# Seven block products in place of eight: Strassen's scheme in the second product of a layer's MLP

## The chip, the cores and the metric

The kernel runs on one core of one Trainium2 chip. Five engines work side by side in a core. PE (TensorE) multiplies matrices: an instruction LDWEIGHTS (PEld in the profile) puts a 128x128 block of weights into the array, and a MATMUL streams up to 512 columns past it into PSUM, an accumulation memory of eight banks with 128x512 f32 each. DVE (VectorE), ACT (ScalarE) and POOL (GpSimd) do element by element work, and SP (SyncE) issues most of the transfers from the device's memory into SBUF, the memory that the engines work in. The metric is the device time in microseconds (us), as the median of several runs.

## The reference

Two transformer layers run over 512 latent tokens and 256 context tokens with a width of 1024: layer 0 mixes tokens by differential attention, layer 1 by neighbourhood attention, and each is followed by an MLP. The change is in the MLP of layer 1, which sees the 512 latent tokens only. Cut to what matters:

```python
D_MODEL = 1024
D_FF = 4 * D_MODEL

def squared_relu_mlp(h, w1, w2):
    return jnp.square(jax.nn.relu(h @ w1)) @ w2

x = x + mod_l[5] * squared_relu_mlp(modulate(rms_norm(x, norm2_g[i]), mod_l[3], mod_l[4]),
                                    w_mlp1[i], w_mlp2[i])
```

So the first product is 512x1024 by 1024x4096, the second 512x4096 by 4096x1024, and the gate `mod_l[5]` multiplies the second one's result before it is added to the stream.

## The kernel before

**Arithmetic.** Every f32 operand of a matrix product is split into a high and a low part of type fp32r, and each product is made of three passes (`PASSES`): high by high, high by low, low by high. The split of a weight block is `wsplit` (L140 to L150): ACT copies the raw block `R` into the high half of a tile `W` (L145), and POOL subtracts that from the raw block to get the low half (L146). One block is 128x1024 f32, 512 KB, fetched by SP (`wraw`, L126 to L130) into one of two raw buffers.

**The MLP** (`mlp`, L809 to L892) walks over 16 chunks of 256 hidden features. `up(c)` (L819 to L845) fetches and splits two blocks of w1, and for each of two tiles of 128 features makes 24 matmuls (8 slices of the width by 3 passes) of 512 tokens into a PSUM tile `D0` or `D1`. ACT applies the relu (L838), DVE squares in place (L839), ACT copies the result into the high half of a tile `H` (L841) and DVE forms the low half (L842). `down` (L856 to L878) fetches and splits two blocks of w2, and for each of four tiles of 128 tokens and each of the two halves `n` of the 1024 output columns makes 6 matmuls (2 features tiles by 3 passes) of 512 columns into a PSUM tile `A` or `B`. DVE adds it to a running sum in SBUF (L874 for the first chunk, L876 after it), one of eight pieces 128x512 that lie three to a tile `Q`.

The loop (L880 to L889) makes chunk c+1's `up` and then chunk c's `down`, so that the hidden values of a chunk are ready long before their `down`. The last two chunks go into one `down` with its flag `end` set: before it, `blend` (L847 to L854) multiplies each piece of the running sum by the gate (DVE, L853) and adds it to the stream (L854: POOL for the left half of the columns, DVE for the right one). The last `down` then makes 12 matmuls for each of the eight pieces, DVE multiplies by the gate (L871), adds to the stream (L872), and ACT's queue sends the result out (L1054).

**Buffers** set when work may begin. In this stage there are four `W` buffers (three opened on the left side and one on the right), two raw buffers `R`, four `N` of 128x1024 (one of them holds the gate), four of the eight `H` (the others hold the MLP's input), and in PSUM one `D0`, one `D1`, two `A` and two `B`. A buffer is given out again when the last reader of what was in it is done: the split of the next weight block waits for the matmuls on the one four blocks earlier.

**Order.** In the attention stages the orders on PE, SP and POOL are written out by hand. In the MLP they are not: a planner lays out each engine's instructions ahead of time. It steps through a timeline of its own estimates, and lets an engine take the instruction that stands earliest in the program among those whose inputs and buffers are ready in that timeline. On the chip each engine then runs its list strictly in that order, and an instruction that has to wait holds up all that stand behind it on its engine.

The stage's loop is

```python
        for c in range(nc_ - 2):
            nxt = up(c + 1)
            side()
            down((c,), hid, False)
```

and `side` does nothing in layer 1.

Of the kernel before, what the change touches and what calls it, by code (L numbers as in the profile page):

```python
# [63 lines left out]
class Block:  # L64
    def __init__(self, tc, ctx, a):
        self.tc = tc
        self.nc = tc.nc
        self.a = a
        self.n = 0
        pool = lambda name, bufs, **kw: ctx.enter_context(tc.tile_pool(name=name, bufs=bufs, **kw))  # L70
        self.const = pool("const", 1)
        self.rpool = pool("rpool", 2)
        self.sb = pool("sb", 1)
        self.dram = pool("dram", 1, space=DRAM)
        self.room, self.turns, self.last = {}, {}, {}


    BUFS = {"H": 8, "Q": 8, "E": 2, "X": 2, "Y": 6, "T": 2, "SQ": 12, "SA": 12, "SO": 8, "C4": 1}
# [46 lines left out]

    def wraw(self, src, n):  # L126

        raw = self.rpool.tile([P, 1024], F32, tag="R", name=self._name("R"))[:, :n]
        self.last["SP"] = self.nc.sync.dma_start(raw, src)
        return raw  # L130

# [21 lines left out]
    def mod_load(self, l, n, early=False):  # L153

        src = self.a["wmod"][l, n]
        if early:
            w = self.sbt('M', [P, 2048])
            self.nc.sync.dma_start(w, src)
            ws = [w]
        else:  # L160
            ws = [self.rpool.tile([P, 1024], F32, tag="R", name=self._name("R")) for s in range(2)]
# [647 lines left out]
    def mlp(self, l, t0, xh, hT, tag, mid, done, side):  # L809
        nc = self.nc  # L810
        a = self.a
        ntok = T - P * t0
        c0 = P * t0
        halves = ((0, 384, 0), (384, 768, 512)) if t0 == 0 else ((256, 768, 0),)
        nx = 2 * (NT - t0)
        acc = [self.sbt(tag[0], [P, 3, 512]) for _ in range((nx + 2) // 3)]
        gate = self.load_gates(l, 1, (0, 1) if t0 == 0 else (0,))

        def up(c):  # L819
            w = [self.wload(a["w1"][l, c, s], 1024) for s in range(2)]  # L820
            hid = []
            for f in range(2):
                ps = self.pst(f'D{f}', (P, 1024))

                cuts = [(o, o + 256, o - c0) for o in range(c0, T, 256)] if c == 0 else halves
                for b0, b1, at in cuts:
                    for kt in range(KT):
                        for p, (x, y) in enumerate(PASSES):
                            o = 256 * (kt % 4) + P * f
                            nc.tensor.matmul(ps[:, at:at + b1 - b0], w[kt // 4][:, x, o:o + P],  # L830
                                             hT[kt][:, y, b0:b1],
                                             start=(kt == 0 and p == 0), stop=(kt == KT - 1 and p == 2))
                r = self.sbt('N', [P, ntok])
                if c and t0 == 0:
                    nc.scalar.activation(r.rearrange("p (h n) -> p h n", h=2),  # L835
                                         ps.rearrange("p (h n) -> p h n", h=2)[:, :, :384], AF.Relu)
                else:
                    nc.scalar.activation(r, ps[:, :ntok], AF.Relu)  # L838
                nc.vector.tensor_mul(r, r, r)  # L839
                u = self.sbt(tag[1], [P, 2, ntok], F32R)  # L840
                nc.scalar.activation(u[:, 0, :], r, AF.Copy)  # L841
                nc.vector.scalar_tensor_tensor(u[:, 1, :], r, 1.0, u[:, 0, :].bitcast(F32),  # L842
                                               op0=ALU.mult, op1=ALU.subtract)
                hid.append(u)
            return hid  # L845

        def blend():  # L847

            for i in range(t0, NT):
                for n in range(2):  # L850
                    j = 2 * (i - t0) + n
                    av = acc[j // 3][:, j % 3, :]
                    nc.vector.tensor_mul(av, av, gate[1 if i < 2 else 0][:, 512 * n:512 * n + 512])  # L853
                    (nc.gpsimd, nc.vector)[n].tensor_add(xh[i, n], xh[i, n], av)  # L854

        def down(cs, hid, end):  # L856
            w = [self.wload(a["w2"][l, 2 * c + f], 1024) for c in cs for f in range(2)]
            if end:
                mid()
            for i in range(t0, NT):  # L860
                for n in range(2):
                    ps = self.pst('A' if end else 'AB'[n])
                    for f, hd in enumerate(hid):
                        for p, (x, y) in enumerate(PASSES):
                            nc.tensor.matmul(ps, hd[:, x, P * i - c0:P * i - c0 + P], w[f][:, y, 512 * n:512 * n + 512],  # L865
                                             start=(f == 0 and p == 0), stop=(f == len(hid) - 1 and p == 2))
                    j = 2 * (i - t0) + n
                    av = acc[j // 3][:, j % 3, :]
                    if end:
                        t = self.sbt('T', [P, 512])  # L870
                        nc.vector.tensor_mul(t, ps, gate[1 if i < 2 else 0][:, 512 * n:512 * n + 512])  # L871
                        nc.vector.tensor_add(xh[i, n], xh[i, n], t)  # L872
                    elif cs[0] == 0:
                        nc.vector.tensor_copy(av, ps)  # L874
                    else:
                        nc.vector.tensor_add(av, ps, av)  # L876
                if end:
                    done(i)  # L878

        nc_ = NFF // 2  # L880
        hid = up(0)
        for c in range(nc_ - 2):
            nxt = up(c + 1)
            side()
            down((c,), hid, False)
            side()
            hid = nxt
        hid += up(nc_ - 1)
        blend()  # L889
        down((nc_ - 2, nc_ - 1), hid, True)  # L890


# [40 lines left out]
def hybrid_block(tc, a, out):  # L933
    nc = tc.nc
    with ExitStack() as ctx, ExitStack() as st:
# [19 lines left out]
        with b.psum_phase("psA", **PS_ATTN0):  # L955
# [65 lines left out]
        with b.psum_phase("psC", **PS_ATTN1):  # L1021
# [25 lines left out]
                run(END1, GROUPS1, heads, load, split, **own)  # L1047
            proj["end"]()
            xh1, hT3 = done
        with b.psum_phase("psD", **PS_MLP1):  # L1050

            def done1(i):
                for n in range(2):
                    nc.scalar.dma_start(out[P * (i - 2):P * (i - 1), 512 * n:512 * n + 512], xh1[i, n])  # L1054

            b.mlp(1, 2, xh1, hT3, 'QH', lambda: None, done1, lambda: None)
        b.close("W", "ST", "W", "N", "VM")

# [69 lines left out]
```

## Time and profile before

| | |
|---|---|
| median of 3 runs | 1906.98 us (1906.21 to 1910.55) |
| the profiled execution's own time | 1907.34 us |
| its span, from the first to the last instruction | 1905.4 us |
| PE busy over the span | 94% |
| DVE, ACT, POOL busy over the span | 59%, 44%, 43% |
| mean granted clock of PE | 0.979 |
| layer 1's MLP | from about 1530 us to the end |
| of it the loop, with PE busy without a gap | 1555.5 to 1874.1 us |

The profile gives one execution of the program on the chip. A row of grouped instructions names line, engine, operation and tiles (`W<-R,W` writes a tile W and reads R and W), and then gives the busy time, the mean of one in ns, and the idle time just before them with what ended it. A row of the timeline starts with the time at which the instruction began and its duration, both in us; a bracket gives the idle time before it and what ended that. A busy engine may be one that waits inside an instruction: a duration that is far above others of the same form is such a wait.

### The profile page before, as it was taken

The page shows a single profiled execution, that of the slowest core. Times are in us where ns is not written, and L with a number is a line of the kernel's source. Part 1 is how long each engine was busy: PE and PEld are TensorE (multiplying, and loading weights), DVE is VectorE, ACT ScalarE, POOL GpSimd, SP SyncE. Part 2 cuts the span into 40 slices and gives each one's busy share as a digit, 9 for nine tenths or more (in the row PEclk, how much of TensorE's full clock was granted, in tenths as well). Part 3 has the DMA queues.
Part 4 walks back from the last instruction along what each step waited for, and adds up shares of the span by engine and source line. Part 5 has one row for each costly group of instructions (what it writes and reads, how often), then busy time and mean ns, then how long its engine had stood idle before and what let it go on. Part 6 is the DMA issues. An engine that isn't in the chain of part 4 may idle for free.

```text
span 1905.4 us, 27130 instructions
## 1 busy us (share of the span) xinstructions
PE 1793.9 (94%) x10256; PEld 1570.9 (82%) x10256; DVE 1132.7 (59%) x2158; ACT 829.2 (44%) x1854; POOL 815.6 (43%) x688
## 2 busy tenths in 40 slices
PE   6989999996999999999999998999998989999998
PEld 5878888885789888888888977998898778888886
DVE  4588777785574343343334676778777664444446
ACT  4476767774342212221221245677667342223321
POOL 3655656653224333342442532344335444444443
PEclk9999999997999999999999998999999999999999
DMA  8122222224324343443432132122112323223232
GB/s 327 43 84 78 87 87 87 89 69 159 119 72 140 130 157 111 166 165 112 157 136 73 56 100 64 56 69 84 56 67 89 116 89 99 89 89 107 92 100 77
DMA packets 66499, 197.61 MB, mean 104 GB/s; under 512 B 8192, under 2 KB 23488, under 8 KB 60224
## 3 DMA queue, kind: packets, MB, share of 16 engines
q1 hardware_dynamic: 58608, 186.03, 29.3%
q10 hardware_dynamic: 7760, 9.85, 1.5%
q8 instruction: 80, 1.31, 0.3%
q14 instruction: 51, 0.42, 0.1%
HBM read 180.74 MB, written 15.11 MB: 103 GB/s over the span
## 4 chain that ended last, share of the span: by engine, by line
PE 75%; DVE 11%; ACT 6%; issue 4%; POOL 2%; DMA 2%; ACTq 0%; SPq 0%; POOLq 0%; DVEq 0%
PE PD L830 22%; PE PA L408 14%; PE PA L865 11%; PE PB L865 9%; PE PA L750 4%; PE PA L257 2%; PE PS L517 2%; PE PB L552 2%; PE PB L701 2%; PE PQ L398 1%; PE PS L656 1%; PE PB L686 1%; ACT E L523 1%; PE PB L541 1%; DVE N L311 1%
## 5 line engine op out<-in xcount | busy, mean ns | idle before, releaser
L146 POOL TENSOR_TENSOR W<-R,W 128x1024 fp32r<-128x1024 f32 x142 | 351.3, 2484 | 541.2 <-ACT W L145 541.0
L830 PE MATMUL PD<-Q,W 128*128 128x384 f32 (+2 forms) x1992 | 395.9, 345 | 2.4 <-DVE Q L334 1.1
L830 PEld LDWEIGHTS PD<-Q,W 128*128 128x128 f32 x1992 | 345.7, 188 | 33.7 <-issue 8.6
L145 ACT ACTIVATE W<-R 128x1024 fp32r<-128x1024 f32 (+1 forms) x172 | 172.6, 1021 | 450.5 <-PE PA L865 193.5
L865 PE MATMUL PA<-W,H 128*128 128x512 f32 x1080 | 275.4, 393 | 4.7 <-POOL W L146 3.0
L865 PEld LDWEIGHTS PA<-W,H 128*128 128x128 f32 x1080 | 200.2, 188 | 51.5 <-issue 4.5
L839 DVE TENSOR_TENSOR N<-N 128x768 f32<-128x768 f32 (+1 forms) x64 | 67.0, 1048 | 279.1 <-ACT N L835 170.3
L865 PE MATMUL PB<-W,H 128*128 128x512 f32 x840 | 209.2, 391 | 0.0
L408 PE MATMUL PA<-W,Q 128*128 128x384 f32 (+1 forms) x1008 | 177.4, 331 | 11.2 <-ACT H L446 11.2
L865 PEld LDWEIGHTS PB<-W,H 128*128 128x128 f32 x840 | 157.4, 188 | 33.3
L408 PEld LDWEIGHTS PA<-W,Q 128*128 128x128 f32 x1008 | 163.0, 196 | 12.9 <-ACT H L446 12.9
L296 POOL TENSOR_TENSOR SQ<-SQ,half 128x4 f32<-128x4 f32 (+1 forms) x96 | 99.2, 1034 | 134.0 <-DVE SQ L421 132.9
L842 DVE SCALAR_TENSOR_TENSOR H<-N,H 128x768 fp32r<-128x768 f32 (+1 forms) x64 | 98.1, 1534 | 25.7 <-ACT H L841 25.0
L408 PE MATMUL PA<-WB,H 128*128 128x384 f32 x576 | 108.4, 340 | 0.8 <-DVE Q L469 0.8
L750 PE MATMUL PA<-W,H 128*128 128x512 f32 x384 | 99.1, 409 | 8.0 <-ACT H L743 5.1
L408 PEld LDWEIGHTS PA<-WB,H 128*128 128x128 f32 x576 | 98.6, 188 | 1.8 <-DVE Q L469 1.1
L830 PE MATMUL PD<-H,W 128*128 128x512 f32 (+1 forms) x408 | 94.1, 378 | 2.5 <-DVE SA L290 2.0
L876 DVE TENSOR_TENSOR H<-PA,H 128x512 f32<-128x512 f32 x78 | 53.9, 690 | 69.6 <-PE PA L865 69.6
L750 PEld LDWEIGHTS PA<-W,H 128*128 128x128 f32 x384 | 73.3, 196 | 26.3 <-ACT H L743 5.4
L830 PEld LDWEIGHTS PD<-H,W 128*128 128x128 f32 x408 | 73.8, 188 | 18.0 <-DVE H L334 2.9
L523 ACT ACTIVATE E<-PS,SA 128x768 f32<-128x768 f32 (+1 forms) x96 | 72.8, 759 | 34.6 <-DVE SA L522 31.9
L517 PE MATMUL PS<-Q,Q 128*128 128x256 f32 (+1 forms) x320 | 69.1, 348 | 19.4 <-ACT Q L446 10.3
(210 smaller groups left out, 3056.5 us busy)
## 6 DMA issues: line engine op xcount, KB each, us to landing
R<-in_w_dram SPq DMA_DIRECT2D x128, 512.0 KB
M<-in_wmod_dram SPq DMA_DIRECT2D x48, 1024.0 KB
R<-in_wqa_dram SPq DMA_DIRECT2D x32, 384.0 KB
R<-in_wqb_dram SPq DMA_DIRECT2D x32, 384.0 KB
Y<-in_rpb_dram SPq DMA_DIRECT2D x48, 128.0 KB
bias<-Y SPq DMA_DIRECT2D x48, 128.0 KB
X<-bias SPq DMA_DIRECT2D x8, 768.0 KB
R<-in_woa_dram SPq DMA_DIRECT2D x8, 512.0 KB
```

Of the source, the lines that this page charges most:

```text
L145: high = nc.scalar.activation(w[:, 0, :n], raw, AF.Copy)
L146: low = (eng or nc.gpsimd).tensor_sub(w[:, 1, :n], raw, w[:, 0, :n].bitcast(F32))
L296: nc.gpsimd.tensor_tensor(r, ss, self.half[:, :n], op=ALU.pow)
L408: nc.tensor.matmul(acc[:, :n], hT[kt][:, x, P * i:P * i + P], w[kt // 2][:, y, o:o + n], start=(kt == 0 and p == 0), stop=(kt == KT - 1 an ...
L517: nc.tensor.matmul(s[:, c0:c1], q[:, m, P * i:P * i + P], k[:, m, c0:c1], start=p == 0, stop=p == 1)
L523: nc.scalar.activation(e[:, m, :nk], s, AF.Exp, bias=mx[:, 0:1], accum_out=sm[:, m:m + 1])
L750: nc.tensor.matmul(ps, oHL[h][:, x, c:c + P], w[h // 2][:, y, 512 * (h % 2):512 * (h % 2) + 512], start=(first and h == hs[0] and p == 0), ...
L830: nc.tensor.matmul(ps[:, at:at + b1 - b0], w[kt // 4][:, x, o:o + P], hT[kt][:, y, b0:b1], start=(kt == 0 and p == 0), stop=(kt == KT - 1 ...
L839: nc.vector.tensor_mul(r, r, r)
L842: nc.vector.scalar_tensor_tensor(u[:, 1, :], r, 1.0, u[:, 0, :].bitcast(F32), op0=ALU.mult, op1=ALU.subtract)
L865: nc.tensor.matmul(ps, hd[:, x, P * i - c0:P * i - c0 + P], w[f][:, y, 512 * n:512 * n + 512], start=(f == 0 and p == 0), stop=(f == len(h ...
L876: nc.vector.tensor_add(av, ps, av)
```

## The change

The running sum over chunks 0 to 13 is now made by pairs of chunks. Call the hidden values of a pair A, a matrix of two by two blocks: two halves of 256 tokens by two chunks of 256 features. The matching rows of w2 are B, two chunks by two halves of 512 columns. The plain way needs eight block products per pair (four blocks of the result, two products each). The change makes seven, by the Winograd form of Strassen's scheme, on sums and differences of blocks, and keeps a running sum of each of the seven products over all pairs. Only at the end (`gathered`) are the four blocks of the result put together from the seven sums. Chunks 14 and 15 go through the last `down` as before.

- One product (`product`) is 2 tiles of 128 tokens by 2 feature tiles by 3 passes, 12 matmuls of 512 columns. A pair takes 7 x 12 = 84 of them, in place of 2 x 48 = 96. Each product adds two pieces to its running sums, 14 per pair and no longer 16; there are 14 pieces to hold and no longer 8, in four `Q` tiles and one `X`.
- The hidden values stay unsplit (`raw_hidden`, one `N` tile for a chunk), since sums of them are formed first: four differences or sums of 128x512 per pair (DVE). Then the seven left operands are split (`split`, ACT and DVE, 128x512 each); before it was four splits of that size.
- The right operands are seven blocks of 128x1024 per pair: four come from differences of raw blocks that DVE makes in place (128x1024 each), and each of the seven is split by ACT and POOL; before it was four. Two blocks are not changed and one is fetched again: seven fetches of w2 per pair where there were four. A fetch (`block`) gathers two runs of 2 KB for each partition.
- Products 1 and 7 (`products_a`) come between `up(c+1)` and `up(c+2)`, and products 5, 6, 3, 4 and 2 (`products_b`) after `up(c+2)`.
- `gathered` adds fourteen operations of 128x512 ahead of `blend`: ten on DVE, four on POOL.
- The raw buffers become four: `b.close("ST")` gives back the attention's staging, and `b.open("right", R=2)` adds two to the two that there were. `self.room["R"]` lets `sbt` hand them out in turn.

The diff, cut to its core:

```diff
-        self.room, self.turns, self.last = {}, {}, {}
+        self.room, self.turns, self.last = {"R": [(self.rpool, 2, None)]}, {}, {}
...
+        def raw_hidden(c):
+            r = self.sbt('N', [P, 2, ntok])
+            for f, ps in up(c):
+                relu2(c, ps, r[:, f, :])
+            return [r[:, :, 128 * nh * t:128 * nh * t + 128 * nh] for t in range(2)]
...
+        def split(src):
+            u = self.sbt(tag[1], [P, 2, 2, 128 * nh], F32R)
+            parts(u, src)
+            return u
+
+        def product(q, u, w, first):
+            for i in range(nh):
+                ps = self.pst('AB'[(q * nh + i) % 2])
+                for f in range(2):
+                    for p, (x, y) in enumerate(PASSES):
+                        nc.tensor.matmul(ps, u[:, x, f, P * i:P * i + P], w[:, y, 512 * f:512 * f + 512],
+                                         start=(f == 0 and p == 0), stop=(f == 1 and p == 2))
+                av = piece(q * nh + i)
...
+                    nc.vector.tensor_add(av, ps, av)
+
+        def products_a(c, r1):
+            b11, b22, b12 = block(c, 0), block(c + 1, 1), block(c, 1)
+            w = self.wsplit(b11, 1024)
+            product(0, split(r1[0]), w, c == 0)
+            nc.vector.tensor_sub(b22, b22, b12)
+            w = self.wsplit(b22, 1024)
+            s3 = self.sbt('T', [P, 2, 128 * nh])
+            nc.vector.tensor_sub(s3, r1[0], r1[1])
+            product(6, split(s3), w, c == 0)
+
+        def products_b(c, r1, r2):
+            b22, b11, b12, b21 = block(c + 1, 1), block(c, 0), block(c, 1), block(c + 1, 0)
+            nc.vector.tensor_sub(b12, b12, b11)
+            nc.vector.tensor_add(r1[1], r1[1], r2[1])
+            w5, u5 = self.wsplit(b12, 1024), split(r1[1])
+            nc.vector.tensor_sub(b11, b22, b12)
+            nc.vector.tensor_sub(r1[0], r1[1], r1[0])
+            product(4, u5, w5, c == 0)
+            w6, u6 = self.wsplit(b11, 1024), split(r1[0])
+            product(5, u6, w6, c == 0)
+            nc.vector.tensor_sub(r1[1], r2[0], r1[0])
+            w3, u3 = self.wsplit(b22, 1024), split(r1[1])
+            product(2, u3, w3, c == 0)
+            nc.vector.tensor_sub(b12, b11, b21)
+            w4, u4 = self.wsplit(b12, 1024), split(r2[1])
+            product(3, u4, w4, c == 0)
+            w2, u2 = self.wsplit(b21, 1024), split(r2[0])
+            product(1, u2, w2, c == 0)
+
+        def gathered():
+            out = {}
+            for i in range(nh):
+                p1, p2, p3, p4, p5, p6, p7 = (piece(q * nh + i) for q in range(7))
+                nc.vector.tensor_add(p6, p1, p6)
+                nc.vector.tensor_add(p7, p6, p7)
+                nc.vector.tensor_add(p6, p6, p5)
+                nc.vector.tensor_add(p3, p6, p3)
+                nc.gpsimd.tensor_add(p2, p1, p2)
+                nc.vector.tensor_sub(p4, p7, p4)
+                nc.gpsimd.tensor_add(p7, p7, p5)
...
+            r1 = raw_hidden(0)
+            for c in range(0, nc_ - 2, 2):
+                r2 = raw_hidden(c + 1)
+                side()
+                products_a(c, r1)
+                side()
+                if c + 2 < nc_ - 2:
+                    nxt = raw_hidden(c + 2)
+                else:
+                    hid = hidden(c + 2)
+                side()
+                products_b(c, r1, r2)
...
+        hid += hidden(nc_ - 1)
         blend()
         down((nc_ - 2, nc_ - 1), hid, True)
...
+        b.close("ST")
+        b.open("right", R=2)
...
+            b.mlp(1, 2, xh1, hT3, 'QH', lambda: None, done1, lambda: None, 'QQQQX')
```

`hidden(c)` is the old `up` with its relu, square and split; layer 0 still goes by it and by the old loop.

More of the change, by code (lines that the diff above doesn't have):

```diff
@@ L126, in wraw @@
     def wraw(self, src, n):
[L128 removed]
+        raw = self.sbt("R", [P, 1024])[:, :n]
         self.last["SP"] = self.nc.sync.dma_start(raw, src)
@@ L160, in mod_load @@
         else:
-            ws = [self.rpool.tile([P, 1024], F32, tag="R", name=self._name("R")) for s in range(2)]
+            ws = [self.sbt("R", [P, 1024]) for s in range(2)]
             for s in range(2):
```

72 lines of the change are left out of this document (46 added, 26 removed).

## The prediction

> **What bounds the kernel now.** I first read the busy time of the engines by stretch, in layer 1's MLP alone (columns: stretch, its length, then for PE, PEld, DVE, ACT and POOL the busy us and instructions, then PE's granted clock, the share of the DMA engines and GB/s).
>
> ```profile
> span 1905.4 us, 27130 instructions
> core 0: us, PE busy (x) PEld busy (x) DVE busy (x) ACT busy (x) POOL busy (x), PEclk, DMA share, GB/s
> 1535.70:1564.00 28.30, 23.05 (x136) 20.60 (x136) 18.98 (x33) 11.01 (x19) 12.04 (x5) 0.88 0.25 78
> 1555.50:1874.10 318.60, 318.60 (x1395) 261.30 (x1394) 156.39 (x182) 91.89 (x117) 145.64 (x62) 1.00 0.30 94
> 1874.10:1883.60 9.50, 6.71 (x25) 4.07 (x23) 6.77 (x7) 3.75 (x5) 5.15 (x2) 1.00 0.19 55
> 1870.00:1905.40 35.40, 27.45 (x115) 20.86 (x113) 20.90 (x23) 3.75 (x5) 8.91 (x4) 0.96 0.24 88
> ```
>
> In the loop PE is busy throughout at the full clock: 1395 matmuls in 318.6 us are 0.2284 us each. The chain of waits says the same; one row of it recurs once per chunk:
>
> ```profile
> 1578.78 9.90 PE PD L830 x43
> ...
> 1842.38 9.91 PE PD L830 x43
> 1854.40 2.50 DVE Q L853
> 1866.75 2.22 DVE X L854
> 1871.54 2.78 DVE E L854
> 1877.04 2.49 DVE N L839
> 1883.64 16.65 PE PA L865 x72
> ```
>
> Twelve chunks lie between the first two rows, 263.6 us, so 21.97 us a chunk and 0.2288 us for each of its 96 matmuls, small gaps included. From 1854 to 1880 the chain leaves PE for DVE rows that are four times as long as the work in them. Why, the timeline tells (start, duration, engine, line):
>
> ```profile
> 1585.33 0.69 DVE L842 SCALAR_TENSOR_TENSOR H<-N,H 128x512 fp32r<-128x512 f32 x1 [0.70 <-ACT H L841]
> 1590.07 0.69 DVE L876 TENSOR_TENSOR Q<-PA,Q 128x512 f32<-128x512 f32 x1
> 1590.34 2.41 POOL L146 TENSOR_TENSOR W<-R,W 128x1024 fp32r<-128x1024 f32 x1 [0.78 <-ACT W L145]
> 1590.81 2.49 DVE L842 SCALAR_TENSOR_TENSOR H<-N,H 128x512 fp32r<-128x512 f32 x1
> ...
> 1623.25 4.76 POOL L146 TENSOR_TENSOR W<-R,W 128x1024 fp32r<-128x1024 f32 x2 [8.54 <-ACT W L145]
> ...
> 1866.67 2.30 DVE L854 TENSOR_TENSOR X<-X,Q 128x512 f32<-128x512 f32 x1
> 1869.65 1.30 POOL L854 TENSOR_TENSOR E<-E,Q 128x512 f32<-128x512 f32 x1 [1.23 <-DVE Q L853]
> 1870.21 1.29 DVE L853 TENSOR_TENSOR Q<-Q,N 128x512 f32<-128x512 f32 x1
> 1870.91 2.86 POOL L146 TENSOR_TENSOR W<-R,W 128x1024 fp32r<-128x1024 f32 x1
> 1871.54 2.78 DVE L854 TENSOR_TENSOR E<-E,Q 128x512 f32<-128x512 f32 x1
> ```
>
> A DVE instruction with both inputs in SBUF takes 0.69 us alone (1585.33) and 2.49 beside a POOL instruction (1590.81): it ends at 1593.30, 0.55 us after POOL's, which ended at 1592.75. DVE works only once POOL is done. The other way round POOL's 1870.91 takes 2.86 us, not 2.41, because DVE's 1870.21, itself held until 1870.95, ran first. So DVE's two-SBUF-input work and POOL's work exclude one another; I call what they share the lock. It is held for 2.38 us by a weight split (4.76 for two), 1.3 us by a POOL add and 0.55 us by a 128x512 operation of DVE. Additions out of PSUM (L876) stay at 0.69 us.
>
> The Trainium skill says this in SBUF — State Buffer, section "Who interferes with whom": a DVE instruction with two SBUF inputs and a GpSimd instruction that reads SBUF take turns, and the later one is fully blocked. The rows above agree (2.49 against 0.69 us). By the loop's row alone (DVE 156.39, POOL 145.64 of 318.6 us) each would have room for what the change adds; by this rule their shares add up, which speaks against the change.
>
> **The change, part by part.**
>
> *Removed.* 12 matmuls of 96 per pair, seven pairs: 84 x 0.2288 = 19.2 us of PE, all on the path. Two PSUM additions per pair go too, beside it and worth nothing.
>
> *Added in the loop, per pair.* The rows for prices not yet shown:
>
> ```profile
> L146 POOL TENSOR_TENSOR W<-R,W 128x1024 fp32r<-128x1024 f32 x55 | 132.1, 2412 | 166.3 <-ACT W L145 166.3
> L145 ACT ACTIVATE W<-R 128x1024 fp32r<-128x1024 f32 x55 | 56.8, 1055 | 142.2 <-PE PB L865 131.9 <-PE PD L830 10.3
> L841 ACT ACTIVATE H<-N 128x512 fp32r<-128x512 f32 x28 | 17.5, 626 | 12.2 <-DVE N L839 12.2
> L838 ACT ACTIVATE N<-PD 128x512 f32<-128x512 f32 x28 | 16.8, 599 | 63.8 <-PE PD L830 63.8
> ...
> L146 DVE TENSOR_TENSOR W<-R,W x30: 951/959/1226, 381.8 to 1410.7; 128x768 fp32r<-128x768 f32 x28, 128x1024 fp32r<-128x1024 f32 x2
> ```
>
> ACT: 11 weight copies, 4 relus, 7 copies: 11 x 1.055 + 4 x 0.60 + 7 x 0.63 = 18.4 us of a pair that should last 180 x 0.2288 = 41.2. Fetches: 11 x 0.524 MB in 41.2 us are 140 GB/s, where the loop now moves 94 and the DMA engines are busy 30%; four raw buffers give each fetch several us. Both are hidden.
>
> The lock: before, 8 weight splits and 8 DVE operations, 8 x 2.38 + 8 x 0.55 = 23.4 of 43.9 us. After, 11 splits, 15 DVE operations of 512 (4 squares, 7 low halves, 4 sums) and 4 differences of 1024 at 1.1 (twice 0.55; the 1.23 us in the last row is the whole instruction): 26.2 + 8.3 + 4.4 = 38.8 of 41.2 us, 94%. It fits, barely. POOL cannot spread its work evenly: a split needs a free W buffer. I went through a pair by the times at which matmuls free the four buffers. Seven splits then come 2.7 us apart from the end of `up(c+2)` on, through `products_b`, and the DVE operations that fall among them delay the last by 3 to 4 us. Each split starts 7 us before its matmuls (buffer free 8.2 to 8.7 us ahead, less ACT's copy) and takes 2.4, which leaves 4.6. So PE mostly doesn't wait. DVE's additions out of PSUM queue behind a blocked operation for up to 2.4 us; four PSUM buffers at 1.37 us each cover 3.4. Bounds: 0 (all cover holds) to 3 us a pair (the lock stands idle that long in each `up`, as POOL's 8.54 us of idle above shows that it can). I take 1 us for the seven together, since cover exceeds delay in this account, and keep 21 as the upper end.
>
> *Added at the end.* This is the larger cost. From 1853.9 to 1874.4 the `blend` runs now (groups by line, count and mean):
>
> ```profile
> L853 DVE TENSOR_TENSOR Q<-Q,N 128x512 f32<-128x512 f32 x8 | 8.4, 1059 | 0.1
> L146 POOL TENSOR_TENSOR W<-R,W 128x1024 fp32r<-128x1024 f32 x3 | 8.1, 2693 | 0.8 <-ACT W L145 0.8
> L854 POOL TENSOR_TENSOR E<-E,Q 128x512 f32<-128x512 f32 x3 | 4.3, 1423 | 3.2 <-DVE Q L853 3.2
> L854 DVE TENSOR_TENSOR E<-E,Q 128x512 f32<-128x512 f32 x2 | 4.2, 2086 | 0.0
> L854 DVE TENSOR_TENSOR X<-X,Q 128x512 f32<-128x512 f32 x2 | 3.0, 1488 | 0.0
> L854 POOL TENSOR_TENSOR X<-X,Q 128x512 f32<-128x512 f32 x1 | 1.3, 1297 | 3.0 <-DVE Q L853 3.0
> L842 DVE SCALAR_TENSOR_TENSOR H<-N,H 128x512 fp32r<-128x512 f32 x1 | 0.7, 679 | 0.0
> ```
>
> Its lock time: 3 x 2.38 + 4 x 1.3 + 13 x 0.55 = 19.5 us in 20.5. The lock is the bound there already. What waits for it is the third and fourth weight block of the last `down`:
>
> ```profile
> 1874.09 3.33 PE L865 MATMUL PA<-W,H 128*128 128x512 f32 x14
> 1876.61 5.15 POOL L146 TENSOR_TENSOR W<-R,W 128x1024 fp32r<-128x1024 f32 x2 [2.84 <-ACT W L145]
> 1879.03 1.95 PE L865 MATMUL PA<-W,H 128*128 128x512 f32 x6 [1.61 <-POOL W L146]
> ```
>
> From 1874.09 to 1883.64 PE does 24 matmuls, 5.5 us of work in 9.5: 4.1 lost. From the third block's split (1876.61) to the unbroken row of 72 matmuls (1883.64) is 7.0 us, then 16.65, then 1905.4 - 1900.3 = 5.1 to the end.
>
> After the change the sums can begin when half of product 6's pieces are added, 4.8 us into the last `products_b` (18 matmuls and one addition). Ahead of the third split the lock then owes: the rest of product 2's split 1.5; two splits for chunk 15 and the first two of the last `down`, 4 x 2.38 = 9.5; eight POOL adds (four of them new) 10.4; and 26 DVE operations (10 sums, 8 gate products, 4 adds, 4 for hidden values) 14.3: 35.7 us. PE in that time has 8.8 us of products, 10.9 of `up(15)` and 2.7 of the last `down`, 22.4. The adds come before the third split in POOL's list, for they stand earlier in the program and in a plan without waits are ready earlier; the last tile's right-hand product and add don't have to precede it (1.1 less). So the third split starts at 4.8 + 34.6 = 39.4. From there as now: 39.4 + 7.0 + 16.65 + 5.1 = 68.2 us from the start of the last `products_b` to the end. Bounds: with the weight splits ahead of the adds only the matmuls and today's 4.1 us count, 24.5 + 9.5 + 16.65 + 5.1 = 55.8; with all the lock's work ahead, at the 95% seen above (35.7 / 0.95), 71.2.
>
> *The sum.* That `products_b` starts after 14 `up`s (672 matmuls), six pairs (504) and products 1 and 7 of the last (24): 1200 x 0.2288 = 274.6 us after 1555.5, so at 1830.1. 1830.1 + 68.2 + 1 for the loop + 1 for the clock = 1900.3 us of span; with the 1.94 us around it (own time 1907.34 less 1905.4) 1902.2, 5.1 below the profiled time. The median is 0.36 below that one, so I forecast 1902 us, 0.26% faster: of 19.2 us some 14 are given back, nearly all at the end.
>
> The 1 us for the clock: the granted clock is 0.96 over the last 35.4 us and 0.88 in the 28.3 us with the entry's gaps, so 1.4 and 3.4 us are lost to it there. A PE that now waits some 12 us falls between (0 to 2 us more).
>
> The Trainium skill, TensorE: Matmul & The Clock Gate, section "What's actually happening", halves the clock after an idle window of about 3.4 us and needs as long of work to give it back; by that the sum has an estimated 1.7 us here, not 1.
>
> **The rivals.** What no measurement of this kernel tells from no change is 0.2%, 3.8 us: 1903.2 to 1910.8.
>
> *The end costs little.* If the planner puts the last weight splits ahead of the adds, the end is the 55.8 us above, and the time 1830.1 + 55.8 + 1.9 = 1888; the postponed adds then hold up the last additions somewhat: 1890. For it: now the first block's split already stands between two adds. Against it: the third did not.
>
> *All of it is given back.* The lock's whole list stands ahead (71.2, +3.0) and the loop loses 0.3 us a pair, 1.1 more than taken: 1906.
>
> *Slower: the lock bounds the loop.* At the 95% reached at the end, 38.8 us are 40.8, against 41.2 of PE. Where the W buffers keep the lock idle for more than 0.4 us a pair, PE waits for weights. POOL now idles 8.54 us at a time for want of a buffer. At 3 us idle a pair lasts 43.8 us, 2.6 too long, seven of them 18: 1902 + 18 - 1 = 1919, the end's 14 us being lost still. It is slower by 0.2% from 1.4 us a pair on (1902 + 9.8 - 1). Against it: 4.6 us of cover for each split.
>
> **How the numbers follow.** Forecast 0.34 (1896 to 1904); cheap end 0.14; all given back 0.24; lock-bound loop 0.28. Nearly all of the first two is faster by over 0.2%: 0.46; within 0.2% 0.25; slower 0.29. The range 1889 to 1918 leaves out the cheap end's best and the loop's worst.
>
> **What would show it.** Right: PE's stretch without a gap lasts to about 1855; a pair takes 41.2 us; POOL's L854-like adds and DVE's sums alternate with durations of 1.3 and 2.5 us; then PE waits 10 us or more for W by POOL before the last 72 matmuls. Wrong: W or PSUM waits in every pair, DVE's additions out of PSUM late by over 3.4 us, or a third split ahead of the adds.

## The result, and the profile after

The changed kernel takes 1918.48 us (median; 1912.88 to 1920.68), before it is 1906.60: a ratio of 1.0057, with a 95% interval of 1.0041 to 1.0072. It is 0.6% slower, where 0.26% faster was forecast; the time lies just over the range (1918).

The matmuls went as announced, 84 fewer. PE's busy time fell by 12.9 us, but the span grew by 5.7. First the head of the page of the changed kernel:

```profile
span 1911.1 us, 27232 instructions
PE 1781.0 (93%) x10172; PEld 1554.5 (81%) x10172; DVE 1262.4 (66%) x2231; ACT 863.8 (45%) x1896; POOL 900.6 (47%) x713
```

Then the busy time of its engines by stretch (columns as in the prediction): the loop, PE's first wait, the last five products, the sums and chunk 15, the waits of the last `down`, and its unbroken row of matmuls.

```profile
1555.50:1834.40 278.90, 273.94 (x1188) 221.68 (x1186) 240.73 (x214) 114.11 (x143) 193.88 (x71) 1.00 0.42 133
1834.40:1838.80 4.40, 0.07 (x2) 0.05 (x1) 3.02 (x2) 2.85 (x6) 4.18 (x2) 1.00 0.32 108
1838.80:1850.70 11.90, 11.87 (x44) 9.30 (x44) 10.34 (x11) 5.17 (x7) 5.61 (x3) 0.86 0.32 108
1850.70:1872.50 21.80, 18.63 (x72) 14.44 (x72) 21.80 (x25) 3.79 (x4) 15.26 (x7) 0.92 0.20 59
1872.50:1886.70 14.20, 5.37 (x13) 2.71 (x12) 14.20 (x9) 2.69 (x4) 12.97 (x8) 0.65 0.00 0
1886.70:1906.30 19.60, 19.53 (x76) 15.16 (x76) 10.04 (x15) 0.00 (x0) 1.67 (x1) 0.90 0.24 89
```

PE is no longer busy throughout in the loop: 278.9 us for 1188 matmuls, where 0.2284 us each would be 271.3. From 1872.5 to 1886.7 it makes 13 matmuls, while DVE is busy the whole time and POOL 12.97 of 14.2 us.

One pair in the timeline shows why. L910 and L903 are a sum and a difference on DVE, L847 the squares, L893 the additions out of PSUM, L146 POOL's weight splits.

```profile
1650.45 2.59 DVE L910 TENSOR_TENSOR N<-N,N 128x512 f32<-128x512 f32 x1
...
1662.37 20.27 POOL L146 TENSOR_TENSOR W<-R,W 128x1024 fp32r<-128x1024 f32 x7 [2.31 <-ACT W L145]
1663.41 5.69 DVE L847 TENSOR_TENSOR N<-N 128x512 f32<-128x512 f32 x2
...
1666.14 1.52 PE L887 MATMUL PB<-W,H 128*128 128x512 f32 x6
...
1669.62 2.29 DVE L903 TENSOR_TENSOR T<-N 128x512 f32<-128x512 f32 x1
...
1670.22 1.52 PE L887 MATMUL PA<-W,H 128*128 128x512 f32 x6
...
1671.84 0.68 DVE L893 TENSOR_TENSOR Q<-PB,Q 128x512 f32<-128x512 f32 x1
...
1672.57 1.66 PE L887 MATMUL PB<-W,H 128*128 128x512 f32 x6 [0.83 <-DVE Q L893]
...
1676.86 1.09 PE L836 MATMUL PD<-Q,W 128*128 128x512 f32 x4
```

POOL's seven splits run without a gap for 20.27 us. Each DVE operation with two SBUF inputs that falls among them waits for one of them to end: two squares take 5.69 us, a difference 2.29. Behind them in DVE's list stand the additions that empty PSUM. The PSUM tile `PB` that PE fills from 1666.14 to 1667.66 is added only from 1671.84 on, 4.2 us later, and PE waits 0.83 us for it. From 1670.22 to 1676.86 PE does four rows of six matmuls in 6.6 us, where 24 x 0.2288 are 5.5. These 1.2 us are all that the pair loses, and they come back in every pair. The waits of PE over the loop (who waited for whom, us in total, times, the longest) name nothing else, and no weight block:

```profile
PE PB L887 <- DVE Q L893: 4.1, 5, 0.8
PE PB L887 <- DVE Q L891: 0.8, 1, 0.8
```

So two of the prediction's signs of being wrong are there: PE waits for PSUM in every pair, and an addition out of PSUM is late by more than the 3.4 us of cover.

At the end, first the wait for an operand of product 5 and then those of the last `down`:

```profile
1819.93 2.59 DVE L910 TENSOR_TENSOR N<-N,N 128x512 f32<-128x512 f32 x1
...
1834.62 5.13 POOL L146 TENSOR_TENSOR W<-R,W 128x1024 fp32r<-128x1024 f32 x2 [3.38 <-ACT W L145]
...
1835.09 2.43 DVE L847 TENSOR_TENSOR N<-N 128x512 f32<-128x512 f32 x1 [0.77 <-ACT N L846]
1837.56 1.67 ACT L850 ACTIVATE H<-N 128x512 fp32r<-128x512 f32 x3 [1.55 <-DVE N L847]
1838.76 0.76 PE L887 MATMUL PA<-W,H 128*128 128x512 f32 x2 [4.33 <-ACT H L850]
...
1878.25 2.79 POOL L146 TENSOR_TENSOR W<-R,W 128x1024 fp32r<-128x1024 f32 x1
...
1881.09 1.34 PE L959 MATMUL PA<-W,H 128*128 128x512 f32 x2 [4.17 <-POOL W L146]
...
1883.51 2.08 PE L959 MATMUL PA<-W,H 128*128 128x512 f32 x4 [1.07 <-ACT H L850]
...
1886.74 19.53 PE L959 MATMUL PA<-W,H 128*128 128x512 f32 x76 [1.16 <-POOL W L146]
```

Product 5's left operand is summed by 1822.5 (L910), but it is split only from 1838.1 on: in ACT's list its copy is the second of the three at 1837.56, behind that of chunk 14's second tile. That one waits for a square, and the square takes 2.43 us instead of 0.69 beside POOL's splits.

The profile above is of the fastest of the four runs (1912.88 us), so the kernel was profiled once more, in a run of 1918.4 us, and the accounts below go by that second profile (experiment 12).

### The profile page after: what moved, and what is told of

The parts are those of the page before. It is cut to its first block, busy times and chain, and to the rows that moved or that the text cites. A ratio compares the mean times of both kernels' runs of the same rounds, so it can differ in the third digit from the quotient of the medians.

```text
span 1911.1 us, 27232 instructions
## 1 busy us (share of the span) xinstructions
PE 1781.0 (93%) x10172; PEld 1554.5 (81%) x10172; DVE 1262.4 (66%) x2231; ACT 863.8 (45%) x1896; POOL 900.6 (47%) x713
## 4 chain that ended last, share of the span: by engine, by line
PE 67%; DVE 16%; ACT 6%; issue 5%; POOL 3%; DMA 2%; ACTq 0%; SPq 0%; DVEq 0%; POOLq 0%
PE PD L836 18%; PE PA L408 15%; PE PA L959 8%; PE PB L959 6%; PE PA L750 3%; DVE N L847 2%; PE PA L257 2%; PE PS L517 2%; PE PB L552 2%; PE PB L887 2%; PE PB L701 2%; POOL W L146 1%; PE PS L656 1%; PE PQ L398 1%; PE PA L887 1%
## 5 line engine op out<-in xcount | busy, mean ns | idle before, releaser
L146 POOL TENSOR_TENSOR W<-R,W 128x1024 fp32r<-128x1024 f32 x163 | 425.0, 2623 | 459.9 <-ACT W L145 456.3
L145 ACT ACTIVATE W<-R 128x1024 fp32r<-128x1024 f32 (+1 forms) x193 | 196.4, 1026 | 434.9 <-PE PA L959 193.6
L847 DVE TENSOR_TENSOR N<-N 128x768 f32<-128x768 f32 (+1 forms) x64 | 96.1, 1510 | 212.1 <-ACT N L843 170.3
L959 PE MATMUL PA<-W,H 128*128 128x512 f32 x744 | 193.4, 400 | 10.9 <-POOL W L146 6.7
L959 PEld LDWEIGHTS PA<-W,H 128*128 128x128 f32 x744 | 138.7, 190 | 46.1 <-POOL W L146 8.7
L408 PEld LDWEIGHTS PA<-W,Q 128*128 128x128 f32 x1008 | 161.7, 195 | 12.9 <-ACT H L446 12.9
L959 PE MATMUL PB<-W,H 128*128 128x512 f32 x504 | 124.0, 392 | 0.0
L959 PEld LDWEIGHTS PB<-W,H 128*128 128x128 f32 x504 | 94.3, 188 | 20.2
L851 DVE SCALAR_TENSOR_TENSOR H<-N,H 128x512 fp32r<-128x512 f32 (+1 forms) x78 | 100.5, 1297 | 13.9 <-ACT H L850 13.9
L750 PE MATMUL PA<-W,H 128*128 128x512 f32 x384 | 98.7, 408 | 7.9 <-ACT H L743 5.1
L750 PEld LDWEIGHTS PA<-W,H 128*128 128x128 f32 x384 | 73.0, 195 | 26.1 <-ACT H L743 5.4
L522 DVE TENSOR_REDUCE SA<-PS 128x1 f32<-128x768 f32 (+1 forms) x96 | 74.5, 776 | 22.0 <-PE PS L517 10.6
L517 PE MATMUL PS<-Q,Q 128*128 128x256 f32 (+1 forms) x320 | 70.5, 354 | 19.2 <-ACT Q L446 9.9
```

Of the source, the lines that this page charges most:

```text
L145: high = nc.scalar.activation(w[:, 0, :n], raw, AF.Copy)
L146: low = (eng or nc.gpsimd).tensor_sub(w[:, 1, :n], raw, w[:, 0, :n].bitcast(F32))
L408: nc.tensor.matmul(acc[:, :n], hT[kt][:, x, P * i:P * i + P], w[kt // 2][:, y, o:o + n], start=(kt == 0 and p == 0), stop=(kt == KT - 1 an ...
L517: nc.tensor.matmul(s[:, c0:c1], q[:, m, P * i:P * i + P], k[:, m, c0:c1], start=p == 0, stop=p == 1)
L522: nc.vector.tensor_reduce(mx, s, op=ALU.max, axis=AX, negate=True)
L750: nc.tensor.matmul(ps, oHL[h][:, x, c:c + P], w[h // 2][:, y, 512 * (h % 2):512 * (h % 2) + 512], start=(first and h == hs[0] and p == 0), ...
```

## The experiments

Each ran on one chip beside the kernel before; its medians there were 1905.7 to 1906.8 us. "Lock" is what DVE's operations with two SBUF inputs and POOL's exclude one another by.

**1. Only leave the matmuls out.** To the kernel before:

```diff
             for i in range(t0, NT):
+                if t0 and not end and cs[0] % 2 and i == NT - 1:
+                    continue
                 for n in range(2):
```

> The kernel before, with nothing of the change except that 12 matmuls (and two additions out of PSUM) of each pair of chunks are left out: the odd chunks of the loop skip the last token tile, so that part of the result is left out. It measures what the saved matmuls are worth alone. All theories: 84 x 0.2288 = 19.2 us less, about 1887.4 us, a pair at 41.2 us. If the loop had a second bound just under PE, less than that.

Measured: 1888.85 us, ratio 0.9913 (0.9898 to 0.9928). The chain of waits (one recurring row, a pair apart), and then the last stretch:

```profile
1598.40 9.90 PE PD L830 x43
1639.62 9.90 PE PD L830 x43
```

```profile
1850.00:1890.00 40.00, 31.53 (x121) 23.46 (x119) 22.90 (x22) 4.35 (x6) 11.18 (x5) 0.86 0.22 79
```

A pair lasts 41.22 us, 2.71 less, as counted. Of 7 x 2.71 = 19.0 us 16.8 arrive in the total; the clock of the last 40 us is 0.86 here. So the saving is real, and the loop has no second bound just under PE as long as nothing else is added.

**2. Take POOL out of the loop.** To the changed kernel, wherever a weight block of this MLP is fetched or split:

```diff
-            w = self.wsplit(b11, 1024)
+            w = self.wsplit(b11, 1024, eng=nc.vector)
```

> The changed kernel, with the low halves of all of this MLP's weight blocks made by DVE (128x1024, 1.1 us) and none by POOL: POOL does nothing in the loop, DVE does more. Theory 'lock' (PE waits because DVE's operations with two SBUF inputs and POOL's exclude one another): no DVE operation is longer than its own work any more, a pair falls from 42.4 us to 41.2 to 41.5, and the end loses 5 to 10 us; about 1918.5 - 7 - 8 = 1903 us. Rival 'DVE is too busy' (35.9 us busy of 41 in the loop now): 11 x 1.1 = 12 us of work more per pair make 48, so a pair takes 48 us and the time is about 1955 us.

Measured: 1899.61 us (1899.26 to 1900.86), ratio 0.9968 (0.9955 to 0.9981). The chain, then one stretch of the loop, then two groups of it:

```profile
1609.22 11.05 PE PD L836 x48
...
1650.38 11.05 PE PD L836 x48
```

```profile
1600.00:1641.00 41.00, 41.00 (x181) 33.68 (x180) 35.10 (x45) 17.71 (x22) 0.00 (x0) 1.00 0.44 141
```

```profile
L146 DVE TENSOR_TENSOR W<-R,W 128x1024 fp32r<-128x1024 f32 x55 | 67.0, 1218 | 13.0 <-ACT W L145 13.0
L910 DVE TENSOR_TENSOR N<-N,N 128x512 f32<-128x512 f32 x5 | 3.4, 683 | 0.0
```

DVE gets 11 operations more per pair, and yet PE has no gap and a pair lasts 41.16 us. L910 takes 0.68 us instead of 2.59. DVE's busy time is the same as in the changed kernel (35.1 against 35.9 of 41 us), only that it works now where it waited before. "DVE is too busy" falls.

**3. Leave the fourteen sums out.**

```diff
-                nc.vector.tensor_add(p6, p1, p6)
...
-                nc.gpsimd.tensor_add(p7, p7, p5)
```

> The changed kernel without the fourteen sums that put the result together (the four running sums 2, 3, 4 and 7 go into the blend as they stand, so the result of the product is not formed). Theory 'lock': 10 x 0.55 + 4 x 1.3 = 10.7 us of lock time go from the end, and the time falls by 8 to 11 us, to about 1909. Rival 'DVE is too busy': only DVE's ten sums count, 6 us. Rival 'the end is lost to the order in which hidden values get their buffers' (4.4 us of PE waiting at 1834 us): less than 2 us.

Measured: 1904.70 us, ratio 0.9997 (0.9987 to 1.0006): 13.8 less than with the sums by the medians, 11.4 by the two ratios, so at the upper end of what theory 'lock' gave or above it, and more than the two rivals. The granted clock differs too (0.92 over the last 35 us here, 0.80 with the sums), so that part of the gain may be clock; this was not separated. This run doesn't tell the lock from DVE's own load.

**4. Give the last pair's operands their buffers first.**

```diff
-                if c + 2 < nc_ - 2:
-                    nxt = raw_hidden(c + 2)
-                else:
-                    hid = hidden(c + 2)
+                nxt = raw_hidden(c + 2)
...
+            hid = []
+            for f in range(2):
+                u = self.sbt(tag[1], [P, 2, ntok], F32R)
+                for t in range(2):
+                    parts(u[:, :, 128 * nh * t:128 * nh * t + 128 * nh], r1[t][:, f])
+                hid.append(u)
```

> The changed kernel, with chunk 14 kept unsplit like the others and split only after the last five products, so that the H buffers go to those products' operands first. Rival 'buffer order': the 4.4 us wait of PE at 1834 us goes, with it the slow clock after it (0.86 over 11.9 us, 1.7 us): 6 us less, 1912. Theory 'lock': during that wait the lock was busy nearly all the time (POOL 4.2 of 4.4 us), so the work only moves on; 0 to 3 us less.

Measured: 1914.34 us, ratio 1.0039 (1.0026 to 1.0051): 4.1 less, between the two numbers. Its stretches:

```profile
1830.00:1850.00 20.00, 19.37 (x85) 15.58 (x83) 20.00 (x17) 11.29 (x16) 15.58 (x6) 1.00 0.27 88
1850.00:1870.00 20.00, 13.92 (x50) 10.94 (x51) 20.00 (x22) 2.72 (x3) 12.34 (x7) 0.83 0.24 79
```

The wait at 1834 is gone, so it hung on the order in which operands get their `H` buffers: planned as it stands, chunk 14's copies stand ahead of product 5's in ACT's list. The lock had a part in it: of the 4.3 us, 1.7 are the square of chunk 14 that was held up beside POOL (2.43 us instead of 0.69). PE now loses 6 us from 1850 on, with DVE busy throughout; 5.8 of them are one wait for an addition out of PSUM. How much of the wait only moved on stays open, as the intervals of the two ratios overlap.

**5. All of it: POOL out of the loop, buffers in order, and no blend.** The `down` with `end` adds the running sum itself:

```diff
+                        if blocks:
+                            nc.vector.tensor_add(t, ps, av)
-                        nc.vector.tensor_mul(t, ps, gate[1 if i < 2 else 0][:, 512 * n:512 * n + 512])
+                        nc.vector.tensor_mul(t, t if blocks else ps, gate[1 if i < 2 else 0][:, 512 * n:512 * n + 512])
                         nc.vector.tensor_add(xh[i, n], xh[i, n], t)
...
-        blend()
+        if not blocks:
+            blend()
+        avs = gathered() if blocks else None
```

> The changed kernel with low halves of this MLP's weights on DVE, chunk 14 unsplit until the last products are through, and no blend: the running sum is added to PSUM in the last down (one DVE addition more per piece, out of PSUM) before the gate, in place of eight products and eight adds ahead of it. Theory 'lock' with the end named as the place of the loss: the loop keeps its 41.2 us a pair and the end falls by 8 us for the blend and 4 for the buffer order: 1899.6 - 12 = 1888 us, near the 1888.9 of the kernel that only leaves 84 matmuls out. If the end were lost to something else (the clock, the fetches), it stays within 4 us of 1899.6.

Measured: 1881.83 us (1879.63 to 1883.03), ratio 0.9875 (0.9859 to 0.9892). It beats both kernels, the one before by 24 us, and is 6 us better than expected; why these 6 stays open. The loop is like that of experiment 2 without a gap of PE:

```profile
1600.00:1800.00 200.00, 200.00 (x877) 164.18 (x876) 173.07 (x217) 86.92 (x108) 0.00 (x0) 1.00 0.44 139
1840.00:1880.00 40.00, 33.13 (x141) 25.55 (x139) 32.56 (x42) 5.31 (x7) 9.12 (x4) 0.96 0.18 66
```

**6. The same with the low halves back on POOL** (the diffs of 4 and 5 without that of 2).

> The same, but with the low halves of the weights on POOL as in the changed kernel. Theory 'lock': the loop is at 42.4 us a pair again, 7 x 1.2 = 8.5 us more than with DVE's low halves, and the fourteen sums still alternate with POOL at the end: about 1888 + 8.5 + 4 = 1900 us. Rival (the loop's loss is DVE's own load): as with the low halves on DVE or faster, 1888 or less, since DVE has 12 us less to do per pair.

Measured: 1901.04 us, ratio 0.9975 (0.9965 to 0.9985): 19.2 us more than in 5, for the choice of the engine alone. A pair lasts 42.4 us again, which is 8.5 of them. The way from the MLP's first transposes (L328) to its unbroken row of 119 matmuls takes 21.8 us instead of 17.6, another 4.1; the rest lies at the end. The rival, by which it would be no slower, falls a second time.

**7 and 8. The two edits on the kernel before.** First the blend taken into the last `down` of layer 1, then the low halves of layer 1's MLP weights on DVE:

```diff
+                        if t0:
+                            nc.vector.tensor_add(t, ps, av)
...
-        blend()
+        if not t0:
+            blend()
```

> The kernel before, with the blend of layer 1's MLP taken into the last down in the same way and nothing else. Theory 'lock': the 4.1 us that PE loses between 1874 and 1884 go, with part of the slow clock behind them: 1902 us. If the blend was hidden, 1906 as before.

```diff
-            w = [self.wload(a["w1"][l, c, s], 1024) for s in range(2)]
+            w = [self.wload(a["w1"][l, c, s], 1024, eng=nc.vector if t0 else None) for s in range(2)]
...
-            w = [self.wload(a["w2"][l, 2 * c + f], 1024) for c in cs for f in range(2)]
+            w = [self.wload(a["w2"][l, 2 * c + f], 1024, eng=nc.vector if t0 else None) for c in cs for f in range(2)]
```

> The kernel before, with the low halves of layer 1's MLP weights on DVE and nothing else: the control for the same edit in the changed kernel. The loop of before has the lock at 53% and PE without a gap, so it stays at 43.9 us a pair by every theory; the end loses less to the lock (6 POOL splits fewer): 1902 to 1906 us. If moving the low halves were worth something by itself, beyond the lock at the end, 1898 or less.

Measured: 1903.21 us without the blend, ratio 0.9988 (0.9978 to 0.9997); 1898.13 us with DVE's low halves, ratio 0.9961 (0.9948 to 0.9974). The second is 7.6 us, at the edge of what I had put down to "worth something by itself". The stretch of the entry, with DVE's low halves and then in the kernel before:

```profile
1530.00:1555.50 25.50, 22.47 (x134) 20.36 (x135) 16.24 (x39) 12.01 (x23) 0.55 (x1) 0.87 0.36 114
```

```profile
1530.00:1555.50 25.50, 18.17 (x121) 16.50 (x121) 18.94 (x40) 11.29 (x22) 9.62 (x4) 0.87 0.29 104
```

PE does 4.3 us more in these 25.5 us. Part of that is only an earlier start: the first transposes begin at 1523.73 here and at 1526.17 in the kernel before, ahead of every split that the edit moves. From there to the row of 119 matmuls it is 16.7 us against 20.6, and 20.6 also in the profiles of experiments 1 and 7, which leave the entry alone. So the edit gains 3.9 us at the entry. There DVE's normalisation and POOL's first weight splits shared the lock, which I had not looked at; an addition of 128x1 shows it, in the kernel before and then with DVE's low halves:

```profile
1537.36 2.32 DVE L308 TENSOR_TENSOR SA<-SA 128x1 f32<-128x1 f32 x1
```

```profile
1535.24 0.15 DVE L308 TENSOR_TENSOR SA<-SA 128x1 f32<-128x1 f32 x1
```

**9. Both edits on the kernel before** (the diffs of 7 and 8).

> The kernel before, with both edits that need nothing of the change: low halves of layer 1's MLP weights on DVE, and its blend taken into the last down. It is what the seven products have to be measured against once both edits are in (1881.8 us with them). If the two edits' gains are the same loss at the end (the lock), they don't add up: about 1897 us, little under the 1898.1 of the low halves alone. If they are independent, 1895.5. The seven products are then worth 14 to 16 us of their 19.2.

Measured: 1899.95 us (1898.58 to 1900.40), ratio 0.9963 (0.9949 to 0.9977). The edits don't add up. Against this kernel the seven products of experiment 5, which also has the buffers in order, are worth 1899.95 - 1881.83 = 18.1 us of the 19.2 counted (16.8 by the two ratios, each known to about 3 us).

**10 and 11. The lock alone.** In experiments 2 and 6 the engine of the low halves changes two things, the lock and how soon a weight block is ready (1.2 us on DVE, 2.4 on POOL). So POOL got work in the kernel of experiment 5 that nobody reads. The diff is that of the half amount, a block's first two quarters; the full one runs over `range(0, n, 256)`:

```diff
+        if 'R' in self.room and len(self.room['R']) == 2:
+            for o in (0, 256):
+                nc.gpsimd.tensor_sub(self.sbt('Y', [P, 256]), raw[:, o:o + 256], w[:, 0, o:o + 256].bitcast(F32))
```

> The fastest kernel so far (seven products, low halves on DVE, chunk 14 split late, no blend) with POOL work beside it that nobody reads: for each weight block of this MLP, POOL subtracts two pieces of 128x256 of the block's high half from the raw block into a spare tile. PE's, DVE's and ACT's own work and the time in which a weight block gets ready stay as they are. Lock time per pair by the rows: 25.2 us of DVE plus 11 x 1.3 to 1.45 of POOL, 39.5 to 41 of 41.2 us. Theory 'lock': DVE operations with two SBUF inputs take up to 0.7 us more and PE waits appear in the loop: a pair rises from 41.16 to some 42 to 43 us. Rival 'POOL was merely a slower and later maker of weight blocks': nothing changes, 41.2 us and 1882.

> The same with four pieces for each weight block, so twice the POOL work that nobody reads. Lock time per pair: 25.2 + 11 x 2.6 to 2.9 = 54 to 57 us. Theory 'lock': the lock is the bound, a pair takes 50 us or more and the kernel 1940 us or more. Rival: as without it, 41.2 us a pair; POOL itself has 29 to 32 us of work in 41.

Measured: 1904.60 us with half, ratio 0.9990 (0.9980 to 1.0001), and 1986.50 us with the full amount, ratio 1.0418 (1.0397 to 1.0438). The chain of the half one, four pairs apart, and then the same 200 us of both, half and full:

```profile
1599.36 7.79 PE PD L839 x34
...
1772.36 7.79 PE PD L839 x34
```

```profile
1600.00:1800.00 200.00, 193.87 (x840) 156.68 (x839) 185.42 (x201) 83.12 (x104) 120.74 (x102) 1.00 0.42 132
```

```profile
1600.00:1800.00 200.00, 172.20 (x690) 134.96 (x689) 158.15 (x161) 61.41 (x79) 186.92 (x164) 0.94 0.35 112
```

A pair lasts 43.25 us with half and 200 / 690 x 180 = 52.2 us with the full amount, where the lock time gave 39.5 to 41 and 54 to 57. PE, DVE and ACT have the same work of their own as in experiment 5, where 877 matmuls ran in these 200 us. The spare work also holds each raw buffer and W buffer until POOL has read it. With half the amount this costs PE nothing that the profile shows: all of PE's waits in these 200 us are for additions out of PSUM, none for a weight block.

```profile
PE PB L890 <- DVE Q L896: 4.6, 4, 1.2
PE PA L890 <- DVE Q L896: 1.5, 4, 0.5
```

So the half amount shows that the lock alone costs PE time in this loop. With the full amount PE waits 29 us there, about half of it for weight blocks, which wait for raw blocks too; how much of its 105 us is the lock's stays open.

**12. The changed kernel once more.**

> The changed kernel as it is, profiled once more: its four runs lie from 1912.9 to 1920.7 us, and the profiled one is the lowest. If the slower ones lose in the loop, a pair takes more than 42.4 us here; if at the end, the third weight split of the last down comes later than 39.5 us after the last five products began, or the granted clock after it is under 0.80 over the last 35 us. If this execution is as fast as the first one, the question stays open.

Measured: 1918.39 us (1916.73 to 1919.49), ratio 1.0059 (1.0036 to 1.0082), and a profile with a span of 1916.6 us (its line numbers are one higher):

```profile
1548.26 19.83 PE PD L837 x119
...
1600.30 10.13 PE PD L837 x44
...
1642.69 10.13 PE PD L837 x44
...
1892.03 19.73 PE PA L960 x76
```

A pair lasts 42.39 us, in the first profile 42.34 (1608.20 to 1650.54 there). The first profile was 4.3 us earlier already at the row of 44 matmuls (1595.99), and of these 3.9 us at the first transposes of layer 1's MLP (1522.56 against 1526.51); the end differs by 1.1 us. So the two differ neither in the loop nor mainly at the end. What sets them apart ahead of the MLP stays open.

## Why the prediction was wrong, point by point

By the second profile and the prediction's own terms (in us of the span; the forecast of 1900.3 holds one us each for the loop and the clock):

| term | forecast | measured |
|---|---|---|
| entry: start of the row of 119 matmuls, against 1546.73 before | 0 | +1.5 |
| loop: lost up to the last five products | 1 | 7.2 |
| wait for product 5's operand | 0 | 4.3 |
| start of the last five products | 1830.1 + 1 | 1843.2 |
| from there to the third weight split of the last `down` | 39.4 | 40.4 |
| from that split to the end | 28.75 + 1 (clock) | 33.1 |
| span | 1900.3 | 1916.6 |

Its timeline at two of these places, then the first of the fourteen sums (from its chain of waits) and POOL's last two adds, and its last stretch:

```profile
1843.17 1.22 PE L888 MATMUL PA<-W,H 128*128 128x512 f32 x2 [4.34 <-ACT H L851]
...
1883.54 2.78 POOL L147 TENSOR_TENSOR W<-R,W 128x1024 fp32r<-128x1024 f32 x1
```

```profile
1852.21 2.06 DVE Q L932
...
1887.56 1.64 POOL L949 TENSOR_TENSOR E<-E,Q 128x512 f32<-128x512 f32 x1 [1.23 <-DVE Q L948]
...
1891.93 1.73 POOL L949 TENSOR_TENSOR E<-E,Q 128x512 f32<-128x512 f32 x1
```

```profile
1881.00:1916.60 35.60, 23.86 (x84) 17.32 (x84) 22.41 (x23) 2.51 (x4) 11.43 (x6) 0.81 0.16 60
```

*The saving, 19.2 us*: right (experiment 1: 2.71 us a pair). The count of fetches is right too, but not for the reason given with the change: of the seven right operands three are raw blocks, and three of a pair's four blocks are fetched a second time.

*The entry* was no term of the prediction. From the first transposes to the row of 119 matmuls it takes 21.75 us here and 20.56 in the kernel before, so 1.2 of the 1.5 us come with the change; from where was not looked at.

*The end as a sum of lock time*: right to 1 us, with the right mechanism, but with luck in the number. The third split came 40.4 us after the start of the last products, with 39.4 forecast. The sums began after 9.0 us (1852.21), not after 4.8, because PE ran its first products at a slow clock (0.77 from 1843.17 to 1854.8) and one addition more stood ahead of them. The list ahead of the split was shorter than the 34.6 us assumed: two of POOL's eight adds and three of the four operations on chunk 15's hidden values came behind it. Counted at the prediction's prices, what did stand ahead is 31.5 us, and from the first sum to the split it is 31.3. So the price of the lock fits, and two errors of 4 and 3 us nearly cancel.

*The step that failed first: "I take 1 us for the seven together."* The loop lost 7.2. The account set one blocked operation of up to 2.4 us against PSUM's cover of 3.4. In the trace blocked operations come in a row, since POOL's splits come in a row: 5.69 us for two squares, then one addition, then 2.29 us for a difference, so that an addition that was due begins 4.2 us late. I had counted the lock's mean demand of 94% and the delay that DVE causes to POOL, and not the delay that a full burst of POOL causes to the DVE list with the additions in it. My bounds (0 to 3 us a pair) held it with 1.2; the choice near the lower one was wrong. At 94% of a shared resource with bursts the middle of the bounds, 10 us, would have been nearer.

*The step that was missing: the order of the buffers in the last pair.* "A buffer is given out again" was in my account of the loop, but I didn't repeat it for the last pair, where two split tiles of chunk 14 claim `H` buffers before product 5's operand: 4.3 us, of which 1.7 are the lock's (experiment 4 removes that wait, and 4.1 us of the time).

*The clock, 1 us.* It cost about 2.2. The last row's 76 matmuls take 19.73 us, where 72 took 16.65 before, so 17.6 at that rate; the granted clock over this row is 0.89, and 1.00 over that of the kernel before. Over the last 35.6 us it is 0.81 as a mean, but for a good part of these PE waits, and there a slow clock costs little. PE waits not once but five times ahead of the last row (0.8, 1.7, 4.2, 1.1 and 1.2 us, 8.9 in all). The rest of the 3.3 us by which the end is too long are four more matmuls in that row (0.9 us) and the way from the third split to it, 8.5 us instead of 7.0.

The Trainium skill (TensorE: Matmul & The Clock Gate, "What's actually happening") gives half the clock after an idle window and full clock after a busy one. The trace agrees in kind: right after the wait at 1838.76 four rows of two matmuls start 0.57 to 0.86 us apart, 0.29 to 0.43 each against 0.23. By one such window it would be 1.7 us, the estimate in the prediction; the last row alone lost 2.2.

*The rivals.* The slower one had the sign and the place right, but not the size: it needed 1.4 us a pair for 0.2%, and the loop lost 1.2. What made the kernel slower by 0.6% is that together with the end's 14 us, the buffer order, the clock and the entry. "The end costs little" didn't happen: six of POOL's eight adds stood ahead of the third split.

Of the sentence from SBUF — State Buffer in the Trainium skill (a two-input DVE operation and a GpSimd one that reads SBUF block each other fully) experiments 2, 6 and 10 are the test: the same DVE instruction takes 0.68 us without POOL and 2.59 beside it, and POOL work that nobody reads costs the kernel 23 us.

## What to carry to other kernels

Before work is added to two engines that exclude one another, add up the time for which each holds what they share, stage by stage, entry and end included. Near the stage's bound expect waits, because the demand comes in bursts (here 94% cost 1.2 us a pair, 53% nothing), and look at what stands behind the blocked instruction in its list. An engine that looks half idle may be the cause: here the slower maker of the low halves was better replaced by the busier one, and the saving of 19 us, lost at first, came through nearly whole (17 to 18 us). And walk the last round of a loop separately, with its own buffers.

## What the runs showed of the hardware that was not expected

Moving work from a half idle engine (POOL, 46% busy in the loop before) to the busier one (DVE, 49%) made the kernel before faster by 7.6 us, though PE had had no gap in that loop: the gain came at the entry and the end. And with five waits of 0.8 to 4.2 us, none of them long, PE's granted clock in the second profile is 0.51 from 1883.0 to 1896.6, 4.6 us into the unbroken row, and 1.00 after that; the 76 matmuls of that row took 0.26 us each instead of 0.23.
